# The first quarter's mixed rows are loaded and halved inside the attention, into the memory of q; the last samples' transpose moves behind the third unit of the output projection

## The chip, the core and the metric

The kernel runs on one core of one Trainium2 chip. The metric is the device time of one execution in microseconds (us). PE is the matrix engine, ACT, DVE and POOL are the scalar, vector and GpSimd engines, SP is the engine that issues most of the transfers (DMAs); ACT issues some of them too. Each engine works through its own instructions in order, and waits on semaphores for the others.

## The reference, cut

One decoder layer for a prompt of 1024 tokens and for 8 samples of 8 new tokens each, with a paged cache of 4096 tokens for every sample. The model width is 1024, the hidden width of the gated feed-forward part (FFN) 2816.

```
def trunk_layer(x, c, ...):
    mod = (jax.nn.silu(c) @ w_ada + b_ada)[:, None, :]
    shift1, scale1, gate1, shift2, scale2, gate2 = jnp.split(mod, 6, axis=-1)
    h = rms_norm(x, norm1) * (1 + scale1) + shift1
    z = h @ w_in                          # q, keys, values, gates, conv and pool inputs
    ...
    o_attn = (g[..., 0:1] * o_cmp + g[..., 1:2] * o_slc + g[..., 2:3] * o_win).reshape(B, T, ATTN_W)
    ...
    x = x + gate1 * (jnp.concatenate([o_attn, y_conv, y_pool], axis=-1) @ w_out)
    h = rms_norm(x, norm2) * (1 + scale2) + shift2
    x = x + gate2 * swiglu(h, w_up, w_down)
    return x, new_kv, win_state, u_ext[:, -CONV_BUF:], p_ext[:, -POOL_BUF:]
```

`o_cmp`, `o_slc` and `o_win` are three attentions (compressed, selected blocks, window). The change concerns the line with `w_out`, and what is ahead of it.

## The kernel before

Tokens lie along the free dimension: 1024 of the prompt and 64 of the samples, T = 1088, cut into four quarters of HALF = 272 (c = 0 to 3). Features lie on the 128 partitions, in KT = 8 blocks (k for inputs, m for outputs).

A product of full precision is made from three fast ones (`mm3`): each factor is halved into a rounded `hi` and the rest `lo`, and hi·hi, hi·lo and lo·hi are summed. `split` halves: a copy on ACT gives hi, a subtraction on DVE (or POOL) gives lo. So every weight and every activation costs work on ACT and on DVE before PE can use it. `w_raw` is a loaded weight, `w_hi` and `w_lo` its halves; `b_hi` and `b_lo` are those of an activation.

The stages, with their place in the profiled execution: the conditioning (adaLN) and the first norm (to 44 us); a part for tokens that gives values and gates (`token_part`, to 77); the input projection (86 to 385); the attention of the prompt, with that of the sample pairs beside it (387 to 819); the output projection (834 to 930); FFN up and down (to the end).

The attention writes its output, the "mixed rows", to `mix_d` in main memory: the prompt's from `mo`, the samples' from `smo`. A pair p of samples ends in `sample_combine`: DVE sums into `co`, PE transposes it, DVE copies it to `smo`, and SP stores it into the last columns of `mix_d`, which belong to the last quarter. The prompt's attention reads the queries `q` (a tile in pool `zq`), halved into `qh` and `ql` by `query_parts` for one of NB = 8 query blocks at a time.

`output_projection` has three groups of quarters: c = 0; c = 1; and c = 2 and 3 together. In each group it goes through the 8 blocks m of output rows; I call one m for one quarter a unit. A unit is 24 matmuls. For each group and m a weight `w_raw` is loaded on SP (`load`), and halved (`split`) into `w_hi` and `w_lo` in two halves of 512. The mixed rows come by `fetch` (`mixc`, 2 blocks k in each transfer; c = 0 on SP, the others on ACT's queue), and `mix` halves them into `mh` and `ml`. The table `MIX` says after which unit how many are halved. `x_load` issues the loads of the residual's x into `x1a` (quarters 0 and 1) or `x1b` (2 and 3) on ACT's queue. After a unit DVE adds the residual (`residual`, into x1a or x1b), SP stores the row (`x_d`), and ACT squares it (`n_ss` or `n_t`) for the second norm. When a quarter's 8 units are done, `late_norm` norms it: a matmul with `mean_d`, `n_rs` with its table load on ACT, a reciprocal on DVE, a multiplication on DVE and a scaling on ACT for each block.

The order of instructions is made when the program is built. Tasks are generators; `run` takes the one with the lowest priority number among those that are due by its own clocks (`use` adds a planned cost to an engine's clock, `yield` gives the time from which the task may go on); `spawn` adds a task, `hold` waits for a condition. A scheduler behind it may still move instructions within what depends on what, so the order of an engine isn't that of the code. Memory comes from pools on a left and a right stack; an instruction that gets memory which another tile held waits for that tile's last use.

## Time and profile before

| | us |
|---|---|
| median of 3 runs | 1679.19 (1678.71 to 1679.51) |
| profiled execution | 1670.79 |
| its span | 1669.2 |
| granted clock of PE, mean | 0.975 |

A row of a timeline has the start in us, the duration in us, the engine, the line of the kernel, the operation, output and inputs, the shape, and how many like it stand in a row; in brackets is how long the engine stood idle just before, and what ended that. The engines' names with q (ACTq, SPq) mean the issue of a transfer. A row of a group of waits has the total, the number and the longest, in us. A row of windows has the stretch, its length, then the busy time of PE, of PE's weight loads, DVE, ACT and POOL, each with its number of instructions, then the granted clock of PE (1.00 is full), the share of the 16 DMA engines that is busy, and GB/s. Durations of PE's matmuls overlap a little, so their starts show the rate.

### The profile page before, as it was taken

Reading aid. Unit: us, or ns where it says so; the run is one execution under the profiler, and the core shown is the slowest. Engines: PE = TensorE matmul, PEld = TensorE weight load, DVE = VectorE, ACT = ScalarE, POOL = GpSimd, SP = SyncE. Lnnn points to the kernel's source line nnn. Section 1 sums busy time; section 2 is a strip of 40 time slices with the busy share of each in tenths; the row PEclk is TensorE's granted clock in tenths of the full one; section 3 lists DMA queues with packets and bytes.
Section 4 is the critical chain, followed back from the end, with each engine's and each line's share of the span. In section 5 each row is a group of like instructions: output and inputs, shape, how many; then the busy total and the mean of one; then the engine's idle time right before and its main releaser. Section 6 shows DMA issues by size and latency. Waiting matters only on the chain. (4 is left out here: it accounts for less than half of the span.)

```text
span 1669.2 us, 35421 instructions
## 1 busy us (share of the span) xinstructions
PE 1565.7 (94%) x12569; PEld 1390.4 (83%) x12569; DVE 1092.0 (65%) x2633; ACT 777.8 (47%) x1829; POOL 660.9 (40%) x789
## 2 busy tenths in 40 slices
PE   6998999997999899899599989999999999899998
PEld 2898897896777666566399989999999999899988
DVE  4713233887555566766589878777777775577695
ACT  3522114335766667666467534433334433344463
POOL 3120110114333223223003366554555554778695
PEclk9999999998999899999899999999999999999999
DMA  9575765325457363344696564346443345966553
GB/s 342 196 261 160 204 174 167 126 101 156 127 178 214 110 193 97 91 127 139 197 323 194 197 215 175 141 145 231 146 143 141 137 145 198 397 232 241 187 168 122
DMA packets 195025, 302.10 MB, mean 181 GB/s; under 512 B 26353, under 2 KB 131378, under 8 KB 194530
## 3 DMA queue, kind: packets, MB, share of 16 engines
q1 hardware_dynamic: 174978, 272.20, 49.4%
q0 software_dynamic: 5856, 16.24, 3.2%
q10 hardware_dynamic: 14016, 11.41, 2.2%
q8 instruction: 100, 1.64, 0.4%
q14 instruction: 75, 0.61, 0.1%
HBM read 233.43 MB, written 70.53 MB: 182 GB/s over the span
## 5 line engine op out<-in xcount | busy, mean ns | idle before, releaser
L139 PE MATMUL bank<-b_hi,w_hi 128*128 128x272 f32 x1232 | 351.4, 290 | 6.0 <-DVE f_g L1677 2.9
L139 PE MATMUL bank<-b_lo,w_hi 128*128 128x272 f32 x1232 | 353.7, 289 | 2.5 <-DVE b_lo L171 2.5
L139 PE MATMUL bank<-b_hi,w_lo 128*128 128x272 f32 x1232 | 348.8, 288 | 0.9 <-DVE w_lo L171 0.9
L139 PEld LDWEIGHTS bank<-b_hi,w_hi 128*128 128x128 f32 x1232 | 230.6, 189 | 9.2 <-ACT b_hi L175 3.8
L139 PEld LDWEIGHTS bank<-b_lo,w_hi 128*128 128x128 f32 x1232 | 232.8, 189 | 3.4 <-DVE b_lo L171 3.3
L139 PEld LDWEIGHTS bank<-b_hi,w_lo 128*128 128x128 f32 x1232 | 230.8, 189 | 1.1 <-DVE w_lo L171 1.1
L1136 POOL TENSOR_SCALAR P<-P,st 128x128 f32<-128x128 f32 (+10 forms) x192 | 108.9, 581 | 229.6 <-DVE st L1132 130.9
L171 DVE TENSOR_TENSOR w_lo<-w_raw,w_hi 128x512 fp32r<-128x512 f32 (+2 forms) x121 | 117.0, 975 | 67.3 <-ACT w_hi L175 66.6
L139 PEld LDWEIGHTS bank<-stream 128*128 128x128 f32 x1056 | 131.1, 203 | 29.0 <-issue 14.6
L171 POOL TENSOR_TENSOR w_s<-w_raw 128x512 f32<-128x512 f32 (+1 forms) x88 | 125.8, 1429 | 67.8 <-DVE w_lo L171 55.2
L139 PE MATMUL bank<-stream 128*128 128x128 f32 x1056 | 138.4, 290 | 11.4 <-DMA wada<-in_wada 6.0
L171 POOL TENSOR_TENSOR x<-x,d_m 128x272 f32<-128x272 f32 x144 | 126.6, 901 | 34.4 <-DVE x L1879 19.6
L175 ACT ACTIVATE w_hi<-w_raw 128x512 fp32r<-128x512 f32 (+2 forms) x122 | 80.7, 677 | 125.9 <-PE bank L139 84.1
L1126 ACT ACTIVATE P<-P,st 128x128 f32<-128x128 f32 (+12 forms) x192 | 112.6, 588 | 44.5 <-DVE st L1120 28.5
L139 PE MATMUL bank<-h_hi,w_hi 128*128 128x384 f32 (+1 forms) x384 | 130.0, 338 | 0.5 <-DVE mod L1024 0.5
L139 PE MATMUL bank<-g,w_hi 128*128 128x272 f32 x616 | 121.6, 293 | 5.7 <-DVE x L1879 5.5
L139 PE MATMUL bank<-h_hi,w_lo 128*128 128x384 f32 (+1 forms) x384 | 126.4, 329 | 0.0
L171 DVE TENSOR_TENSOR w_lo<-w_s,w_hi 128x512 fp32r<-128x512 f32 (+1 forms) x124 | 116.3, 940 | 14.6 <-ACT w_hi L175 12.6
L139 PE MATMUL bank<-h_lo,w_hi 128*128 128x384 f32 (+1 forms) x384 | 125.7, 327 | 0.0
L139 PE MATMUL bank<-g,d_hi 128*128 128x272 f32 x616 | 120.3, 292 | 4.2 <-DVE x L1879 3.1
L1879 DVE SCALAR_TENSOR_TENSOR x<-bank,mod,x 128x272 f32<-128x272 f32 (+1 forms) x192 | 87.0, 476 | 38.3 <-PE bank L139 33.9
L139 PEld LDWEIGHTS bank<-g,w_hi 128*128 128x128 f32 x616 | 98.1, 191 | 7.3 <-DVE x L1879 6.1
(373 smaller groups left out, 3720.9 us busy)
## 6 DMA issues: line engine op xcount, KB each, us to landing
g_d<-f_s SPq DMA_DIRECT2D x57, 544.0 KB, 3.1
g<-g_d SPq DMA_DIRECT2D x56, 544.0 KB, 6.1
wada<-in_wada SPq DMA_DIRECT2D x96, 256.0 KB, 5.3
stream<-in_cacheA SPq DMA_DIRECT2D x192, 128.0 KB, 3.2
w_raw<-in_wup SPq DMA_DIRECT2D x40, 512.0 KB, 4.4
unit<-in_cacheB SPq DMA_DIRECT2D x152, 128.0 KB, 2.4
stream<-in_cacheB SPq DMA_DIRECT2D x104, 128.0 KB, 2.4
w_raw<-in_wout SPq DMA_DIRECT2D x24, 512.0 KB, 4.8
```

What stands on the lines that cost most here:

```text
L139: return self.nc.tensor.matmul(out, lhsT, rhs, start=start, stop=stop, skip_group_check=chain)
L171: (self.nc.vector if eng == "dve" else self.nc.gpsimd).tensor_tensor(out, a, b, op=op)
L175: self.nc.scalar.activation(hi, src, AF.Copy)
L1126: nc.scalar.activation(Ps, Ps, AF.Exp, scale=-1.0, bias=sy[:, g, 0:1], accum_out=sy[:, g, 1:2])
L1136: nc.gpsimd.tensor_scalar(Ps, Ps, sy[:, g, 3:4], 0.0, op0=OP.mult, op1=OP.add)
L1879: nc.vector.scalar_tensor_tensor(out[:, :n], acc[:, :n], self.mod[:, 5, m, 0:1], out[:, :n], op0=OP.mult, op1=OP.add)
```

## The change

One tile of 17,408 bytes on each partition, with the tag "q", now lies in a pool `base` that is open for the whole program, and serves in turn the first x (`x0`), the queries `q`, the mixed rows of the first quarter (`mix0`, both halves of 8 blocks), those of the third quarter (`mix2`), and from the third quarter's norm on the small tiles of the FFN (`hidden_space`: stores, sums and shares that had pools of their own).

A new task `first_mix` runs in the attention: when the last query block has been halved and the prompt's values have reached 14 units, it loads `mix0` in two transfers on SP and halves the 8 blocks. `output_projection` fetches quarters 1 to 3 only, the second on SP; it has 9 buffers of `mh` and `ml` where it had 17; the third quarter's rows go to `mix2`, in one go when the first quarter has been used. The transpose, copy and store of the last sample pair (`sample_store`, with `co` and `smo` in `base`) come after the third unit (m = 2) of the first quarter. The adaLN weights have 14 buffers, before 16. Pools in `tail` are opened in another order.

```diff
@@ -892,9 +892,8 @@
             yield from self.token_part(tp, h)
-        zq_ = self.pool("zq", "left")
-        self.q = zq_.__enter__().tile([P, 4, T], F32, name="q")
-        self.zout = (zq_, zp_)
+        self.q = self.big("q").rearrange("p (r t) -> p r t", r=4)
+        self.zout = (zp_,)
         order = ["kc", "vc", "cg0", "ch0", "bg0", "cg1", "ch1", "bg1", "p0", "ks", "p1", "kw", "q0", "q1", "q2", "q3"]
@@ -1057,6 +1056,7 @@
         self.split(*self.qs, self.q[:, :, j * P:(j + 1) * P], 512)
+        self.q_parts = j + 1
@@ -1422,23 +1422,29 @@
             nc.vector.tensor_scalar(w[:, a:b], w[:, a:b], ds_[:, 2 + x:3 + x], None, op0=OP.mult)
-        o = pool.tile([P, P], F32, name="co", bufs=2)
+        o = pool.tile([P, P], F32, name="co", bufs=2) if p < 3 else self.co
         nc.vector.tensor_scalar(o, part[:, 11], gr[:, 0:1], None, op0=OP.mult)
...
             nc.vector.scalar_tensor_tensor(o, part[:, c], w[:, c:c + 1], o, op0=OP.mult, op1=OP.add)
-        yield self.use("dve", 4.0, self.t["pe"]) + 0.5
-        tr = yield from self.bank_of("S")
+        r = self.use("dve", 4.0, self.t["pe"]) + 0.5
+        if p < 3:
+            yield r
+            tr = yield from self.bank_of("S")
+            self.sample_store(p, tr, o, pool.tile([P, 4, 2, NT], F32, name="smo", bufs=2))
+            self.give("S", self.t["dve"])
+        self.combined = p + 1
+
+    def sample_store(self, p, tr, o, mo):
+        nc = self.nc
         self.tr(tr[:, 0:P], o)
-        mo = pool.tile([P, 4, 2, NT], F32, name="smo", bufs=2)
         for g in range(2):
...
                 tr[s, 0:P].rearrange("p (b g r t) -> p g b r t", b=2, g=2, r=4)[:, g])
-        self.give("S", self.use("dve", 0.4, self.t["pe"]))
+        self.use("dve", 0.4, self.t["pe"])
         nc.sync.dma_start(self.mix_d[:, 0:4, SEQ + 16 * p:SEQ + 16 * p + 16],
                             mo.rearrange("p r b t -> p r (b t)"))
-        self.combined = p + 1
@@ -1459,6 +1465,23 @@
         self.spawn(lambda: 2 + 1.1 * self.u_done / 36, self.sample_attention(sp))
+        self.spawn(1.95, self.first_mix())
+
+    def first_mix(self):
+        nc = self.nc
+        yield from self.hold(lambda: self.q_parts == NB and self.v_done >= 14)
+        mix = self.big("mix0", F32R).rearrange("p (k x t) -> p k x t", k=KT, x=2)
+        for k in range(0, KT, 4):
+            nc.sync.dma_start(mix[:, k:k + 4, 1].bitcast(F32), self.mix_d[:, k:k + 4, 0:HALF])
+        at = self.use("dma", 3.0, self.t["pe"]) + 2.5
+        yield at
+        for k in range(KT):
+            hi, lo = mix[:, k, 0], mix[:, k, 1]
+            src = lo.bitcast(F32)
+            nc.scalar.activation(hi, src, AF.Copy)
+            r = self.use("act", 0.09 + HALF * 0.00084, at)
+            self.mix0.append((hi, lo, self.combine(lo, src, hi.bitcast(F32), OP.subtract, HALF, r, "dve")))
+            yield self.mix0[-1][2]
@@ -1473,6 +1496,9 @@
+    def big(self, name, dt=F32):
+        return self.base.tile([P, 4 * T], dt, name=name, tag="q", bufs=1)
+
     def halves(self, a):
@@ -1494,7 +1520,8 @@
         todo = [m for _ in groups for m in range(KT)]
-        raw, ws, mx, parts = [], [], [], {}
+        raw, ws, mx, mix2 = [], [], [], []
+        parts = {(0, k): a for k, a in enumerate(self.mix0)}
@@ -1505,33 +1532,36 @@
-        order = [(c, k) for c in range(4) for k in range(0, KT, 2)]
+        order = [(c, k) for c in range(1, 4) for k in range(0, KT, 2)]
...
                 t = pool.tile([P, 2, HALF], F32, name="mixc", bufs=4)
-                (nc.sync if c == 0 else nc.scalar).dma_start(t, self.mix_d[:, k:k + 2, c * HALF:c * HALF + HALF])
+                (nc.sync if c == 1 else nc.scalar).dma_start(t, self.mix_d[:, k:k + 2, c * HALF:c * HALF + HALF])
                 mx.append((c, k, t, self.use("dma", 0.8, self.t["pe"]) + 2.2))
...
                 c, k0, t, at = mx.pop(0)
+                if (c, k0) == (2, 0):
+                    mix2.append(self.big("mix2", F32R).rearrange("p (k x t) -> p k x t", k=KT, x=2))
                 for k in range(2):
-                    hi = pool.tile([P, HALF], F32R, name="mh", bufs=17)
-                    lo = pool.tile([P, HALF], F32R, name="ml", bufs=17)
+                    if c == 2:
+                        hi, lo = mix2[0][:, k0 + k, 0], mix2[0][:, k0 + k, 1]
+                    else:
+                        hi = pool.tile([P, HALF], F32R, name="mh", bufs=9)
+                        lo = pool.tile([P, HALF], F32R, name="ml", bufs=9)
                     r = self.split(hi, lo, t[:, k], HALF, at)
...
-        fetch()
         load()
-        for _ in range(3):
-            fetch()
         load()
         split()
-        mix(4)
         load()
+        for _ in range(4):
+            fetch()
         xq = [(c, k) for c in range(4) for k in range(4)]
@@ -1551,7 +1581,10 @@
                         wk = [self.halves(a)[:, k % 4] for a in w[k // 4][:2]]
-                        self.mm3(acc[:, :HALF], wk, parts[c, k][:2], k == 0, k == KT - 1)
+                        last = self.mm3(acc[:, :HALF], wk, parts[c, k][:2], k == 0, k == KT - 1)
+                    if c == 0 and m == 2:
+                        with self.tc.issue_after(last.ins):
+                            self.sample_store(3, self.bank(), self.co, self.smo)
                     if c == cs[-1]:
@@ -1565,9 +1598,22 @@
+    def hidden_space(self):
+
+        big = self.big("f_sT", F32R)
+        v = [big[:, 4 * HALF * x:4 * HALF * (x + 1)] for x in range(4)]
+        self.f_s = [a.rearrange("p (a b c) -> p a b c", a=2, b=2) for a in v[:3]]
+        self.f_T = [a.rearrange("p (a b) -> p a b", a=2).bitcast(F32) for a in (v[3][:, 0:2 * HALF], v[3][:, 2 * HALF:])]
+        self.f_U = [a.rearrange("p (a b) -> p a b", a=2).bitcast(F32) for a in (v[2][:, 0:2 * HALF], v[2][:, 2 * HALF:])]
+        self.x13 = {(c, h): v[2].bitcast(F32)[:, HALF * (2 * c + h):HALF * (2 * c + h + 1)] for c in range(2) for h in range(2)}
+        self.d_m = [big[:, HALF * n:HALF * (n + 1)].bitcast(F32) for n in range(6)]
+        self.b_t = [v[1].bitcast(F32)[:, HALF * n:HALF * (n + 1)] for n in range(3)]
+
     def late_norm(self, nt, ch, x1, ss, ready):
         nc = self.nc
+        if ch == 2:
+            self.hidden_space()
         c0, n = QUARTERS[ch]
@@ -2108,8 +2163,8 @@
                 self.ada_setup(ap)
-                begin(np_, 0, lambda: np_.tile([P, KT, CHUNKS[0][1]], F32, name="x0"))
-                ada = self.ada_rounds(ap, (1, 0), 16, nc.sync, "b")
+                begin(np_, 0, lambda: self.big("x0")[:, 0:KT * CHUNKS[0][1]].rearrange("p (k t) -> p k t", k=KT))
+                ada = self.ada_rounds(ap, (1, 0), 14, nc.sync, "b")
                 t = next(ada)
...
```

The rest of the diff gives other tiles their places in the shared memory (`hidden_space`: the FFN's stores, sums and shares, and x of the third quarter as the norm writes it) and opens pools in another order.

Three places show how the instructions move. The first is the start of the output projection, on PE from the attention's last matmuls on (`unit` is gathered keys or values of a sample, `spt` transposed weights of its softmax). Before:

```order
L143 MATMUL bank<-ident,e 128x128 x8
L139 MATMUL bank<-unit,spt 64x128 x16
L143 MATMUL bank<-ident,co 128x128
L139 MATMUL bank<-mh,w_hi 128x272 x5
L139 MATMUL bank<-ml,w_hi 128x272
L139 MATMUL bank<-mh,w_lo 128x272
L139 MATMUL bank<-mh,w_hi 128x272
```

and now (`mix_9074` is the tile mix0; the transpose of `co` stands 45 rows on, behind the third unit):

```order
L143 MATMUL bank<-ident,e 128x128 x8
L139 MATMUL bank<-unit,spt 64x128 x16
L139 MATMUL bank<-mix_9074,w_hi 128x272 x2
L139 MATMUL bank<-mix_9074,w_lo 128x272
L139 MATMUL bank<-mix_9074,w_hi 128x272 x2
L139 MATMUL bank<-mix_9074,w_lo 128x272
L139 MATMUL bank<-mix_9074,w_hi 128x272 x2
```

The output projection's matmuls follow the attention's, with mix0 in the place of mh and ml, and the transpose has gone from between them.

At the same place ACT, from the first weights of the output projection on. Before:

```order
L175 ACTIVATE w_hi<-w_raw 128x512 x2
L161 ACTIVATE part<-bank 128x128
L175 ACTIVATE w_hi<-w_raw 128x512 x7
L1540 DMA x1a_10498<-in_xT 128x2x272 x3
L175 ACTIVATE mh<-mixc 128x272 x2
L1540 DMA x1a_10498<-in_xT 128x2x272
L175 ACTIVATE mh<-mixc 128x272 x2
L1540 DMA x1a_10499<-in_xT 128x2x272
L1514 DMA mixc<-mix_d 128x2x272
L1540 DMA x1a_10499<-in_xT 128x2x272
```

and now:

```order
L175 ACTIVATE w_hi<-w_raw 128x512 x2
L161 ACTIVATE part<-bank 128x128
L175 ACTIVATE w_hi<-w_raw 128x512 x6
L1570 DMA x1a_10517<-in_xT 128x2x272 x4
L410 ACTIVATE n_ss<-x1a_10517 128x272
L175 ACTIVATE mh<-mixc 128x272 x4
L1570 DMA x1a_10518<-in_xT 128x2x272
L410 ACTIVATE n_t<-x1a_10517 128x272
L1570 DMA x1a_10518<-in_xT 128x2x272
L410 ACTIVATE n_t<-x1a_10517 128x272
L175 ACTIVATE mh<-mixc 128x272 x2
L175 ACTIVATE w_hi<-w_raw 128x512 x2
```

ACT's copy of the fifth unit's weights, the last row now, stands behind six issues of x1a, three squares (`n_ss`, `n_t`) of finished rows and six copies to mh. Before, nine weight halves stood together ahead of the issues and the copies to mh.

The second place is ACT where the second quarter begins. Before:

```order
L175 ACTIVATE mh<-mixc 128x272 x3
L1514 DMA mixc<-mix_d 128x2x272
L175 ACTIVATE mh<-mixc 128x272
L410 ACTIVATE n_t<-x1a_10498 128x272
L175 ACTIVATE w_hi<-w_raw 128x512 x2
L1514 DMA mixc<-mix_d 128x2x272 x2
L175 ACTIVATE w_hi<-w_raw 128x512 x2
L410 ACTIVATE n_ss<-x1a_10499 128x272
L175 ACTIVATE mh<-mixc 128x272
L1578 ACT_TABLE_LOAD
L1578 ACTIVATE n_rs<-bank,eps 128x272
```

and now (`mix_10959` is the tile mix2; the first row has the weights of the first quarter's last unit and of the second's first):

```order
L175 ACTIVATE w_hi<-w_raw 128x512 x4
L175 ACTIVATE mix_10959<-mixc 128x272 x8
L410 ACTIVATE n_t<-x1a_10517 128x272
L1541 DMA mixc<-mix_d 128x2x272
L175 ACTIVATE w_hi<-w_raw 128x512 x2
L1541 DMA mixc<-mix_d 128x2x272 x3
L410 ACTIVATE n_ss<-x1a_10518 128x272
L1624 ACT_TABLE_LOAD
L1624 ACTIVATE n_rs<-bank,eps 128x272
L1641 ACTIVATE x1a_10517<-x1a_10517,mod,s_129 128x272
L175 ACTIVATE w_hi<-w_raw 128x512 x2
```

Eight copies to mix2 stand in a row between the weights, and the norm's table load and n_rs come ahead of the weights in the last row. Before, the copies to mh were spread over the units.

The third is ACT in the attention (`P` and `e` are softmax weights of the prompt and of a sample, `cw` factors of a sample's parts, `pt` transposed P), as one piece of the difference:

```order
 L1378 ACTIVATE e,den<-e,nm 128x512
 L1417 ACTIVATE cw<-nm,cs 128x2
-L1126 ACTIVATE P,st<-P,st 128x55 x3
+L1481 ACTIVATE mix_9074<-mix_9074 128x272 x4
+L1126 ACTIVATE P,st<-P,st 128x55 x2
+L1481 ACTIVATE mix_9074<-mix_9074 128x272 x4
+L161 ACTIVATE pt<-bank 128x8x64
+L1126 ACTIVATE P,st<-P,st 128x55 x2
 L1126 ACTIVATE P,st<-P,st 128x896 x2
```

Eight copies to mix0 stand among the softmax steps of one query block; on DVE eight subtractions follow them.

At the start of the input projection, which isn't shown, the first loads of its weights (`w_raw<-in_win`) move on SP behind two loads of FFN weights that are prepared ahead (`p_raw`) and one store of their halves (`w_d`).

More of the change, by code (lines that the diff above doesn't have):

```diff
@@ L1614, in operands @@
         yield max(at) - 1.0
-        B = {(h, c): x1["at"](2 * p + c, i + 4 * h) for h in range(2) for c in range(2)}
+        B = {(h, c): x1["out"](2 * p + c, i + 4 * h) for h in range(2) for c in range(2)}
         B11, B12, B21, B22 = B[0, 0], B[0, 1], B[1, 0], B[1, 1]
@@ L2017, in tail @@
         p0 = p0_.__enter__()
+        xb_ = [self.pool(f"x1b{i}") for i in range(4)]
+        xb = {}
+        for i in (2, 1, 0, 3):
+            pool = xb_[i].__enter__()
+            xb[i] = pool.tile([P, 2, 2, HALF], F32, name="x1b")
         nt_ = self.pool("nt")
         nt = nt_.__enter__()
-        xb_ = [self.pool(f"x1b{i}") for i in range(4)]
-        xb = {}
-        for i in reversed(range(4)):
-            pool = xb_[i].__enter__()
-            xb[i] = pool.tile([P, 2, 2, HALF], F32, name="x1b")
+        bt_ = self.pool("bt")
+        bt = bt_.__enter__()
+        bt = [bt.tile([P, HALF], F32, name=f"b_t{n}") for n in range(3)]
         xa_ = self.pool("x1a")
@@ L2033, in x_load @@
             return xb[i][:, c - 2], xT[:, :, i, c * HALF:c * HALF + HALF]
-        x1 = {"load": x_load, "at": lambda c, k: xa[c][:, k] if c < 2 else xb[k % 4][:, c - 2, k // 4]}
+        at = lambda c, k: xa[c][:, k] if c < 2 else xb[k % 4][:, c - 2, k // 4]
+        x1 = {"load": x_load, "at": at, "out": lambda c, k: self.x13[c - 2, k // 4] if c > 1 and k % 4 == 3 else at(c, k)}
         def first_pair():
@@ L2145, in build @@
         self.constants()
+        self.base = self.ctx.enter_context(self.pool("base", "left"))
+        self.co = self.base.tile([P, P], F32, name="co3")
+        self.smo = self.base.tile([P, 4, 2, NT], F32, name="smo3")
         st_ = self.pool("stream", "left")
```

35 lines of the change are left out of this document (20 added, 15 removed).

## The prediction

> **What bounds the kernel.** The page comes first: which engine is full.
>
> ```profile
> span 1669.2 us, 35421 instructions
> PE 1565.7 (94%) x12569; PEld 1390.4 (83%) x12569; DVE 1092.0 (65%) x2633; ACT 777.8 (47%) x1829; POOL 660.9 (40%) x789
> ```
>
> PE bounds it with 94%, so a change that leaves its matmuls as they are can win only from the 103.5 us in which it stands, or from a slow clock. The profiled execution took 1670.79 us, 1.6 more than its span and 8.4 (0.5%) less than the median of 1679.19; my sum is a difference against the profiled execution, and I add it to the median. A change under 0.2% (3.4 us) can hardly be told from none here.
>
> Second, the waits of PE from 816 to 1000 us (total, times, longest):
>
> ```profile
> PE bank L139 <- ACT mh L175: 8.4, 1, 8.4
> PE bank L143 <- DVE co L1428: 6.9, 1, 6.9
> ```
>
> Two waits lead the list. PE's timeline shows that they stand side by side, where the attention ends and the output projection begins:
>
> ```profile
> 816.70 1.97 PE L139 MATMUL bank<-unit,spt 128*64 128x128 f32 x32 [0.65 <-DVE cs L1422]
> 825.54 0.47 PE L143 MATMUL bank<-ident,co 128*128 128x128 f32 x1 [6.87 <-DVE co L1428]
> 834.46 1.50 PE L139 MATMUL bank<-mh,w_hi 128*128 128x272 f32 x5 [8.45 <-ACT mh L175]
> 837.55 0.29 PE L139 MATMUL bank<-mh,w_hi 128*128 128x272 f32 x1
> ```
>
> From 818.67 to 834.46 PE does one transpose of 0.47: 15.3 us idle. What mh waits for is in ACT's timeline, with DVE's half of the first weights below, and the columns of the windows (PE, PEld, DVE, ACT, POOL, clock, DMA share, GB/s) show the price in clock:
>
> ```profile
> 818.07 1.15 ACT L175 ACTIVATE w_hi<-w_raw 128x512 fp32r<-128x512 f32 x2
> ...
> 823.87 1.15 ACT L175 ACTIVATE w_hi<-w_raw 128x512 fp32r<-128x512 f32 x2 [2.40 <-DMA w_raw<-in_wout]
> 833.97 0.43 ACT L175 ACTIVATE mh<-mixc 128x272 fp32r<-128x272 f32 x1 [6.79 <-DMA mixc<-mix_d]
> ```
> ```profile
> 818.74 0.68 DVE L171 TENSOR_TENSOR w_lo<-w_raw,w_hi 128x512 fp32r<-128x512 f32 x1
> ```
> ```profile
> 830.00:835.00 5.00, 0.54 (x2) 0.55 (x3) 0.56 (x2) 1.02 (x3) 0.00 (x0) 0.50 1.06 342
> 835.00:840.00 5.00, 5.00 (x33) 5.00 (x32) 2.57 (x7) 1.98 (x6) 0.00 (x0) 0.75 0.97 294
> 845.00:850.00 5.00, 5.00 (x42) 5.00 (x41) 3.98 (x9) 2.75 (x7) 0.00 (x0) 1.00 1.10 372
> 860.00:865.00 5.00, 5.00 (x42) 5.00 (x41) 4.99 (x13) 4.58 (x12) 0.00 (x0) 1.00 0.98 304
> 875.00:880.00 5.00, 4.66 (x37) 4.42 (x36) 5.00 (x12) 5.00 (x12) 0.00 (x0) 1.00 0.61 196
> 890.00:895.00 5.00, 3.94 (x29) 3.63 (x29) 4.86 (x11) 2.74 (x6) 0.00 (x0) 1.00 0.74 231
> ```
>
> The mixed rows come last, behind weights. After the gap the clock is 0.50, then 0.75. A warm window holds 42 matmuls in 5 us, 0.12 each, so a unit (one block of 128 output rows for one quarter: 24 of them) takes 3.0 us; the window at 0.75 has 9 fewer, and with the ten slow ones up to 837.55 I put the slow clock at 1.9. Before, the first quarter's eight units end at 834.46 + 1.9 + 24 = 860.4. Beyond that PE is full but for 0.34 and 1.06 (the windows at 875 and 890), DMA is full to 865, and DVE from 860: little there has slack.
>
> **The change, part by part.**
>
> *The gap goes.* Mixed rows of the first quarter are in memory, and the last samples' transpose stands behind the third unit. PE's first unit needs only w_hi (from 818.07) and w_lo (to 819.4; its first product is third in line): PE can start about 819.1, so 0.4 is left. Gain −15.3 −1.9 = −17.2; cost 0.4. The transpose's copy and store then have nobody on PE behind them until the third quarter.
>
> *The weights are next.* Weights for units 1 to 3 (counted from 0) come as before: the last at 823.87 + 1.15 = 825.0, while PE needs it at 819.1 + 9.0. Unit 3 ends, transpose included, at 831.5. In the new order ACT's half of unit 4's weights stands behind four issues of x1a, a square that needs unit 0's residual (so the first x1a must have landed), six copies to mh of the second quarter, and two more squares. Issue to landing of the transfers there (count, KB, median):
>
> ```profile
> w_raw<-in_wout SPq DMA_DIRECT2D x9, 512.0 KB, 4.6
> x1a<-in_xT ACTq DMA_DIRECT2D x8, 272.0 KB, 5.2
> x1b<-in_xT ACTq DMA_DIRECT2D x7, 272.0 KB, 7.0
> mixc<-mix_d ACTq DMA_DIRECT2D x6, 272.0 KB, 6.3
> ...
> mixc<-mix_d SPq DMA_DIRECT2D x4, 272.0 KB, 5.2
> ```
>
> 825.1 + 5.2 for x1a, 0.5 residual, 0.4 square, six copies and two squares at 0.35 to 0.43: 834.3 at the earliest, 836.2 if x1a lands in 7.0 as x1b does; with the half of 0.6, PE stands 3.4 to 5.4. I take 4.4. Unit 7 has the same trouble: on SP its w_raw stands behind four mixc, the finished rows of units 0 to 3 and the transposed output, and on ACT its w_hi stands behind eight x1b issues and a mixc, each of which waits for an earlier landing (5.2 to 7.0 apiece, overlapping). From 834.5 two rounds of these end at 847 to 848.5; units 4 to 6 end about 845: 3.8 (2 to 5). DMA's share above (1.06 to 1.10) says why I don't take the low end: the first quarter's 1.1 MB of mixc no longer loads here, which at 342 GB/s relieves 3.3 us, but x1a, x1b and weights want the same 16 engines 15 us sooner. So the first quarter ends 17.2 − 8.6 = 8.6 earlier, at T = 851.8.
>
> *The second quarter starts with a pile.* The third quarter's rows go into the shared memory, which the first quarter's occupy until T: sixteen halvings in one go, ahead of unit 1's weights on both ACT and DVE; and the first quarter's norm follows. Their rows today:
>
> ```profile
> 861.32 1.38 ACT L175 ACTIVATE mh<-mixc 128x272 fp32r<-128x272 f32 x4
> ...
> 866.29 1.28 ACT L1578 ACT_TABLE_LOAD   x1
> 867.58 0.49 ACT L1578 ACTIVATE n_rs<-bank,eps 128x272 f32<-128x272 f32 x1
> ```
> ```profile
> 861.53 0.49 DVE L1468 SCALAR_TENSOR_TENSOR x1a<-bank,mod,x1a 128x272 f32<-128x272 f32 x1
> ...
> 862.54 1.49 DVE L171 TENSOR_TENSOR ml<-mixc,mh 128x272 fp32r<-128x272 f32 x4
> ...
> 868.31 1.84 DVE L1581 RECIPROCAL n_rs<-n_rs 128x272 f32<-128x272 f32 x1
> ...
> 870.96 0.78 DVE L1587 TENSOR_TENSOR x1a<-x1a,n_rs 128x272 f32<-128x272 f32 x2
> ```
>
> Eight copies are 2 × 1.38 = 2.8 on ACT, eight differences 3.0 on DVE; then a square, w_hi, w_lo: unit 1 resumes at T + 4.7, where PE was ready at T + 3.0: 1.7. After its own w_hi (T + 4.2) ACT does a square, the table load and n_rs, to T + 6.4; DVE follows with the reciprocal to T + 8.2, seven multiplications (2.7) and a residual to T + 11.3, and only then with unit 2's w_lo: T + 11.7, where unit 1 ended at T + 7.5: 4.2. Unit 4 waits another 1.4 behind copies to b_hi. Sum 7.3 (bounds 1.4, if the norm's steps find room while PE works, and 9). Unit 4 then ends at T + 15 + 7.3 = 874.1 and before at 860.4 + 15 = 875.4: 1.3 of the 8.6 are left.
>
> *Clock.* Each new wait can slow what follows. The trace has two near rows, with the windows behind them:
>
> ```profile
> 692.48 1.21 PE L143 MATMUL bank<-ident,P 64*128 64x64 f32 x32 [2.60 <-POOL P L1136]
> 968.95 0.56 PE L139 MATMUL bank<-b_hi,w_hi 128*128 128x272 f32 x1 [2.95 <-DVE f_g L1677]
> ```
> ```profile
> 692.00:696.00 4.00, 3.48 (x52) 2.52 (x52) 2.58 (x10) 2.07 (x4) 0.43 (x1) 1.00 0.50 153
> 970.00:975.00 5.00, 5.00 (x27) 5.00 (x27) 4.69 (x8) 1.29 (x3) 4.62 (x7) 0.60 0.17 60
> ```
>
> After 2.60 the clock stays at 1.00; after 2.95 the window has 27 matmuls and not 42: 15 × 0.12 = 1.9 lost. Three of the new waits (4.4, 3.8, 4.2) are longer. Unit 4's loss is hidden, since unit 7 waits for a transfer anyway; unit 7's counts, 1.9; the second quarter's is hidden but for 0.5 by unit 4's wait of 1.4. I take +2.4, bounds 0 and 5.7 (all three). [...]
>
> *Later waits.* Of 0.34 + 1.06, which come of DVE and ACT being late, I count 1.0 as gone, since eight differences (3.0) have left DVE: −1.0, bounds −1.4 and 0.
>
> *Attention pays for the halving.* The two loads overwrite q, so they follow its last read:
>
> ```profile
> 675.94 0.69 DVE L171 TENSOR_TENSOR ql<-q,qh 128x512 fp32r<-128x512 f32 x1
> ```
> ```profile
> 679.08 0.28 ACT L1417 ACTIVATE cw<-nm,cs 128x2 f32<-128x2 f32 x1
> ```
>
> Issued at 676.6 and landed in about 4 (under w_raw's 4.6, as DMA is nearly idle here), they hold ACT from 679.4 to 680.6: 1.2. Then come eight copies (2.8) between softmax steps, and eight differences among DVE's steps that end in the wait of 2.60 above. DVE is full there, and DMA at 0.03:
>
> ```profile
> 684.00:688.00 4.00, 4.00 (x36) 2.73 (x34) 3.96 (x17) 4.00 (x11) 1.50 (x3) 0.59 0.03 6
> ```
>
> DVE comes some 3.4 late (3.0 and a little waiting). PE's wait for POOL grows by 0.5, if this work fills waits of ACT and DVE, to 4.0, if all of it and part of the load's landing reach PE; I take 2.1, near the middle. Nothing gives it back, as PE goes on in order.
>
> *Input projection.* Its first weight loads lie in other memory now, wait for the token part's last matmuls, and stand behind two p_raw and one w_d on SP. PE has other work meanwhile:
>
> ```profile
> 77.35 4.63 PE L139 MATMUL bank<-c_peT,stream 128*128 128x2 f32 x32
> 81.84 4.95 PE L139 MATMUL bank<-stream 128*128 128x128 f32 x22
> 86.53 0.43 PE L139 MATMUL bank<-h_hi,w_hi 128*128 128x384 f32 x1
> ```
>
> Issued at 77.4, landed in 4.6 as w_raw's row above, halved in about 2.3 (ACT's two halves take 1.15, and DVE as long): 84.3. PE needs them at 86.53, and 1.6 later still, since seven more of the 22 transposes of 4.95 now stand ahead. Cost 0; bounds 0 and +4, if a w_d ahead lands late.
>
> The adaLN weights' 14 buffers instead of 16, hidden_space's fixed places for tiles that had pools, and the removal of pool zq leave PE's work; I take 0 ± 1.
>
> Sum: −17.2 + (0.4 + 4.4 + 3.8) + 7.3 + 2.4 − 1.0 + 2.1 + 0 = +2.2, so 1673.0 for the profiled execution and 1681.4 for the median.
>
> **The rivals.**
>
> *Half of the new waits only.* If x1a lands in 4.6 or less, unit 4 waits 2 and unit 7 1, and clock costs 0.5, attention its low end 0.5, the second quarter still 7.3: −17.2 + 3.4 + 7.3 + 0.5 − 1.0 + 0.5 = −6.5, 1673. For it: 1.1 MB less to move. Against: DMA at 1.06.
>
> *The whole gain stays.* The planner's order is harmless since DVE and ACT start their piles while PE is busy; second quarter 1.4: −17.2 + 0.4 + 1.4 + 2.1 − 1.0 = −14.3, 1665. For it: ACT is busy only 2.75 of 5 us at 845. Against: the transfers' landing times.
>
> *Slower: the clock falls after every new wait.* The place is units 4 and 7, unit 2 of the second quarter, and the attention's POOL wait grown from 2.60 to 4.7. Price: 5.7 + 1.9 instead of 2.4, so +7.4: 1686.6. It decides when these waits pass 2.95 with nothing behind that waits anyway. For it: the row at 968.95; against: later transfers hide part. [...]
>
> *Slower: the input projection waits.* Decided when the halves are later than 88.1, that is, with a landing of over 8 us: +2.2 + 4, 1685.4. Against: 4.6 above.
>
> *The gap stays,* because the early rows or the first weights come late after all: no gain and no waits in the first quarter, 7.3 − 1.0 + 2.1 = +8.4, 1688. Weights ready at 819.1 speak against it.
>
> **How the numbers follow.** Base case 0.42, 1681.4, rounded to 1681 (own range 1677 to 1685); half of the waits 0.22; whole gain 0.15; clock 0.11; input projection 0.07; gap stays 0.03. Faster by over 0.2% (under 1675.8): 0.20 of the second case and the 0.15: 0.35. Slower (over 1682.6): 0.10 of the base, 0.11, 0.07, 0.03: 0.31. The rest 0.34. The range leaves out the whole gain and the gap that stays, and takes the other ends: 1669 to 1687.
>
> **What would show it.** Right: no wait of over 1 us before the first matmul with mix; waits for w_hi or w_lo of 3 to 5 us some 12 us and 25 us later, and of 4 us in the second quarter; clock under 0.8 after them; a wait for POOL of 4 to 5 near 692. Wrong: PE full from 819 to 860, which would make it much faster; or a wait for the first input projection's weights near 86.

## The result, and the profile after

The changed kernel takes 1690.27 us (median of 7 runs, 1685.69 to 1694.20) beside 1678.71 for the kernel before (7 runs, 1671.17 to 1680.22): a ratio of 1.0074, 95% interval [1.0051, 1.0097]. Run again, beside 27 runs of the kernel before on the chip of the last experiments, it took 1687.96 beside 1675.08, 1.0079 [1.0056, 1.0102]. It is 12 to 13 us slower, where I had said +2.2.

The profiled execution took 1693.83 us, 3.6 above its median, and that of before 1670.79 lay 4.3 under the median of 27 later runs (1675.08; lowest 1669.33, highest 1684.40). So these two traces lie 23.0 us apart, some 10 us more than the kernels do, and I read every place in a second profile of the changed kernel (1687.42 us) too. The page, first and second profile:

```profile
span 1692.2 us, 35415 instructions
...
PE 1585.9 (94%) x12569; PEld 1401.9 (83%) x12569; DVE 1082.3 (64%) x2631; ACT 779.0 (46%) x1830; POOL 662.6 (39%) x790
```
```profile
span 1685.8 us, 35415 instructions
...
PE 1578.4 (94%) x12569; PEld 1395.8 (83%) x12569; DVE 1084.3 (64%) x2631; ACT 779.9 (46%) x1830; POOL 663.3 (39%) x790
```

PE's matmuls are as many as before. It stands idle for 106.3 and 107.4 us, before 103.5: taking the gap of 15.3 us away left PE as idle as it was. The rest of the time lies in PE's busy time, in part because its mean clock is lower (0.968 and 0.972, before 0.975). By the starts of landmarks in PE's timelines (us):

| stretch | before | changed, 1st | changed, 2nd |
|---|---|---|---|
| to the token part's first matmul | 44.65 | 49.28 | 48.50 |
| to the input projection | 41.9 | 43.5 | 42.0 |
| input projection and attention | 732.1 | 741.1 | 737.1 |
| output projection | 116.4 | 121.3 | 121.7 |
| FFN | 734.2 | 737.1 | 736.5 |

The place of the change, PE's timeline, in the first profile and then in the second:

```profile
831.89 1.97 PE L139 MATMUL bank<-unit,spt 128*64 128x128 f32 x32 [0.65 <-DVE cs L1422]
...
834.68 0.39 PE L139 MATMUL bank<-mix,w_lo 128*128 128x272 f32 x1 [0.21 <-DVE w_lo L171]
...
850.50 0.82 PE L139 MATMUL bank<-mix,w_hi 128*128 128x272 f32 x2 [3.68 <-ACT w_hi L175]
868.61 0.82 PE L139 MATMUL bank<-mix,w_hi 128*128 128x272 f32 x2 [5.79 <-ACT w_hi L175]
877.75 0.39 PE L139 MATMUL bank<-mh,w_hi 128*128 128x272 f32 x1 [0.61 <-ACT w_hi L175]
...
883.92 0.39 PE L139 MATMUL bank<-mh,w_hi 128*128 128x272 f32 x1 [1.94 <-ACT w_hi L175]
885.87 0.39 PE L139 MATMUL bank<-mh,w_lo 128*128 128x272 f32 x1 [1.44 <-DVE w_lo L171]
```
```profile
825.62 1.97 PE L139 MATMUL bank<-unit,spt 128*64 128x128 f32 x32 [0.65 <-DVE cs L1422]
...
844.15 0.82 PE L139 MATMUL bank<-mix,w_hi 128*128 128x272 f32 x2 [3.60 <-ACT w_hi L175]
862.41 0.82 PE L139 MATMUL bank<-mix,w_hi 128*128 128x272 f32 x2 [6.22 <-ACT w_hi L175]
```

The gap is gone: 0.21 us are left of it. Unit 4 waits 3.68 and 3.60, unit 7 waits 5.79 and 6.22, both for ACT's half of the weights. What the waits cost in clock (the columns as in the prediction):

```profile
849.00:854.00 5.00, 3.28 (x12) 2.79 (x13) 5.00 (x13) 3.97 (x10) 0.00 (x0) 0.54 1.09 374
854.00:859.00 5.00, 5.00 (x33) 5.00 (x33) 2.82 (x6) 1.33 (x3) 0.00 (x0) 0.77 1.01 330
...
869.00:874.00 5.00, 5.00 (x25) 4.77 (x25) 2.09 (x4) 1.12 (x3) 0.00 (x0) 0.57 0.78 242
```

At 0.12 us apiece, 15, 9 and 17 matmuls are missing beyond the idle time. ACT ahead of unit 7's weights, and the transfers there with count, KB and median us to landing:

```profile
858.82 0.43 ACT L410 ACTIVATE n_t<-x1a 128x272 f32<-128x272 f32 x1 [2.99 <-issue]
...
862.87 0.43 ACT L410 ACTIVATE n_t<-x1a 128x272 f32<-128x272 f32 x1 [3.62 <-DMA x1b<-in_xT]
862.90 4.67 ACTq L1570 DMA_DIRECT2D x1b<-in_xT  x3
867.61 0.43 ACT L410 ACTIVATE n_t<-x1a 128x272 f32<-128x272 f32 x1 [4.31 <-DMA x1b<-in_xT]
867.95 2.17 ACT L175 ACTIVATE w_hi<-w_raw 128x512 fp32r<-128x512 f32 x4
```
```profile
x1a<-in_xT ACTq DMA_DIRECT2D x8, 272.0 KB, 6.1
x1b<-in_xT ACTq DMA_DIRECT2D x8, 272.0 KB, 6.8
mixc<-mix_d SPq DMA_DIRECT2D x4, 272.0 KB, 7.5
```

From 859.25 to 867.95 ACT computes two squares of 0.43 and no more. Three issues of x1b hold its queue for 4.67 us until earlier x1b have landed, and the halving behind them comes the moment they let go. DMA is full meanwhile (a share of 1.06). Landing takes 6.1 us for x1a (5.2 before), 6.8 for x1b (7.0 before) and 7.5 for mixc on SP (5.2 before).

### The profile page after: what moved, and what is told of

Same layout as the page of the kernel before. It is cut to its first block, busy times and chain, and to the rows that moved or that the text cites. A ratio compares the mean times of both kernels' runs of the same rounds, so it can differ in the third digit from the quotient of the medians.

```text
span 1692.2 us, 35415 instructions
## 1 busy us (share of the span) xinstructions
PE 1585.9 (94%) x12569; PEld 1401.9 (83%) x12569; DVE 1082.3 (64%) x2631; ACT 779.0 (46%) x1830; POOL 662.6 (39%) x790
## 4 chain that ended last, share of the span: by engine, by line
PE 65%; DVE 12%; ACT 6%; DMA 6%; issue 5%; POOL 3%; SPq 1%; ACTq 0%; DVEq 0%; POOLq 0%
PE bank L139 62%; PE bank L143 3%; ACT P L1126 2%; DVE P L1114 2%; DVE w_lo L171 1%; DMA w_raw<-in_wup 1%; POOL w_s L171 1%; DMA w_raw<-in_wout 1%; POOL x L171 1%; DMA x1b<-in_xT 1%; DVE co L1428 1%; ACT w_hi L175 1%; POOL f_sT L171 1%; DMA stream<-in_wtok 1%; DMA wada<-in_wada 1%
## 5 line engine op out<-in xcount | busy, mean ns | idle before, releaser
L1136 POOL TENSOR_SCALAR P<-P,st 128x128 f32<-128x128 f32 (+11 forms) x192 | 109.4, 584 | 229.1 <-DVE st L1132 107.7
L139 PEld LDWEIGHTS bank<-stream 128*128 128x128 f32 x1056 | 135.9, 209 | 30.1 <-issue 17.0
L139 PE MATMUL bank<-stream 128*128 128x128 f32 x1056 | 143.3, 296 | 12.2 <-DVE pre L551 5.5
L171 POOL TENSOR_TENSOR x<-x,f_sT 128x272 f32<-128x272 f32 x144 | 127.3, 906 | 38.3 <-DVE x L1928 27.6
L1126 ACT ACTIVATE P<-P,st 128x640 f32<-128x640 f32 (+12 forms) x192 | 112.7, 588 | 44.1 <-DVE st L1120 28.3
```

The lines of the kernel that those rows point to most:

```text
L139: return self.nc.tensor.matmul(out, lhsT, rhs, start=start, stop=stop, skip_group_check=chain)
L171: (self.nc.vector if eng == "dve" else self.nc.gpsimd).tensor_tensor(out, a, b, op=op)
L1126: nc.scalar.activation(Ps, Ps, AF.Exp, scale=-1.0, bias=sy[:, g, 0:1], accum_out=sy[:, g, 1:2])
L1136: nc.gpsimd.tensor_scalar(Ps, Ps, sy[:, g, 3:4], 0.0, op0=OP.mult, op1=OP.add)
```

## The experiments

All ratios are against runs of the kernel before on the same chip (its medians there 1675.1 to 1675.2). A stretch's time is that of one profile; only ratios have intervals.

**Changed kernel, the residual's loads of the last two quarters later.** `x_load` issues x1b only in the second quarter, behind ACT's last halving copy.

```
-                    x_load()
+                    if cs[0] == 0:
+                        x_load(2 if xq and xq[0][0] < 2 else 0)
+                    else:
+                        with self.tc.issue_after(self.last_act.ins):
+                            x_load()
```

> The changed kernel, with the loads of x1b (third and fourth quarter) issued on ACT in the second quarter, behind its weight halves, and not in the first. Theory B2 (the first quarter's second wait, 5.8 us, is made by x1b: its issues hold ACT, and its 2.2 MB hold the DMA engines, while the last units' weights are needed): that wait falls under 1.5, no long wait comes in its place, and the time falls by 4 to 6 from the changed kernel, ratio to before 1.004. Rival C (what is won there is given back in the second quarter, as with x on POOL's queue, where a wait of 9.5 came up): a wait of 5 or more in the second quarter, and at most 1 us less, ratio 1.007.

1678.42, ratio 1.0016 [1.0002, 1.0031]: some 10 us of the 12 to 13 are gone, more than the 4 to 6 expected. PE's timeline, and the windows of both waits:

```profile
846.85 0.82 PE L139 MATMUL bank<-mix,w_hi 128*128 128x272 f32 x2 [3.15 <-ACT w_hi L175]
861.03 0.52 PE L139 MATMUL bank<-mix,w_hi 128*128 128x272 f32 x2 [1.57 <-ACT w_hi L175]
```
```profile
845.00:850.00 5.00, 2.93 (x10) 2.44 (x11) 5.00 (x13) 4.31 (x11) 0.00 (x0) 0.65 1.08 379
...
860.00:865.00 5.00, 3.76 (x28) 3.54 (x29) 3.54 (x6) 3.56 (x7) 0.00 (x0) 1.00 0.71 210
```

Unit 4's wait stays, since x1a and mixc are still ahead of it; unit 7's falls from 5.79 to 1.57. The output projection takes 110.8 us, not 121.3: 10.5, of which 4.4 to unit 7 (30.3 us behind the attention's end, before the edit 34.8) and the rest later; the FFN gives 2.7 to 3.3 of it back (739.8 us). Single waits differ between executions, so all profiles count here. With x1b early (the two above, and the run by tiles below, whose output projection is the same) the first quarter takes 40.1, 40.0 and 36.7 us and the rest of the output projection 81.1 to 81.7; with x1b late (this run and two below that have it) they take 33.9 to 34.8 and 76.9 to 77.2. That the early x1b makes most of the loss is shown, in the first quarter and behind it.

**Changed kernel, x1a and x1b issued on POOL's queue.** The rival was that ACT's queue alone is to blame, and not what the 16 DMA engines have to carry.

```
-                nc.scalar.dma_start(dst, src)
+                nc.gpsimd.dma_start(dst, src)
```

> The changed kernel, with the loads of x1a and x1b issued on POOL's queue and not on ACT's; ACT's order then has ten weight halves in a row where six stood ahead of the loads. Theory B (the first quarter's two waits of 3.7 and 5.8 us, and the slow clock behind them, come from weight halves that stand on ACT behind the issues of x and the squares): both waits shrink under 1.5, the first quarter takes some 28 us and not 39.5, and the time falls by 8 to 12, to 1679 to 1682. Rival C (the transfers themselves are the limit there, and the waits turn into waits for landed weights): at most 3 less, 1687 or more.

1687.18, 1.0070 [1.0052, 1.0089]: nothing gained that this can tell. The waits of the first quarter fell to 0.66 and 0.49, and it took 27.5 us, as theory B had it; but a larger wait came in the second quarter, and the time is rival C's. PE, then ACT and SP there:

```profile
866.79 0.59 PE L139 MATMUL bank<-mh,w_hi 128*128 128x272 f32 x1 [9.53 <-ACT w_hi L175]
```
```profile
860.74 4.95 ACTq L1541 DMA_DIRECT2D mixc<-mix_d  x4
865.79 0.43 ACT L410 ACTIVATE n_ss<-x1a 128x272 f32<-128x272 f32 x1 [4.66 <-DMA w_raw<-in_wout]
866.12 1.13 ACT L175 ACTIVATE w_hi<-w_raw 128x512 fp32r<-128x512 f32 x2
```
```profile
858.23 0.33 SPq L1515 DMA_DIRECT2D w_raw<-in_wout  x1
```

Now four mixc hold ACT for 4.95 us, and the unit's weights were issued only at 858.23. The wait has moved, the bytes to load are the same, and the DMA engines' share is 0.98 to 1.07 in the windows from 845 to 860, where it was 0.98 to 1.09 in the changed kernel.

**Changed kernel, the last transpose at its old place.** The sample pair's transpose and store again follow its sums.

```
-                    if c == 0 and m == 2:
-                        with self.tc.issue_after(last.ins):
-                            self.sample_store(3, self.bank(), self.co, self.smo)
...
```

> The changed kernel, with the last samples' transpose at its old place, ahead of the first unit. Theory D (weights and x set the pace of the first quarter, so PE's start matters little): PE stands some 7 us before the first unit again, the first quarter's two waits shrink by about as much, and the time rises by 0 to 3 from the changed kernel. Rival (the wait adds to the others): 6 to 8 more.

1685.12, 1.0065 [1.0049, 1.0080], not to be told from the changed kernel. PE waits ahead of the output projection instead:

```profile
831.79 0.48 PE L143 MATMUL bank<-ident,co 128*128 128x128 f32 x1 [6.83 <-DVE co L1428]
```

Behind it no wait over 0.21 is left in the first quarter: in that time, by my reading, the loads land and ACT gets ahead. So the wait for the sums and the waits for weights stand for each other. In its profile the output projection takes 114.3 us, 7 less than in the changed kernel, and the FFN 742.5, 5 to 6 more; of the 7 nothing sure is left in the time.

**Kernel before, the transpose behind the third unit.** This part of the change alone.

> The kernel before, with only the transpose, copy and store of the last samples moved behind the third unit of the first quarter (their two tiles, 768 bytes, in the pool of constants). Theory D: the first quarter's rows are issued on SP some 2 us earlier, as they no longer stand behind the samples' store, the gap before the first unit is 12 to 13 us instead of 15, and the time falls by 1 to 2. Rival (the rows come late because DMA is full, not because of the queue): no change.

1677.27, 1.0012 [0.9995, 1.0029]. The gap shrinks to 12.57, as expected, but the time doesn't fall: what the gap saves is lost in the second quarter (30.6 us, before 25.1). PE, DVE's run of multiplications of the norm, and a window there:

```profile
830.32 1.05 PE L139 MATMUL bank<-mh,w_hi 128*128 128x272 f32 x3 [12.57 <-ACT mh L175]
```
```profile
867.82 4.23 DVE L1596 TENSOR_TENSOR x1a<-x1a,n_rs 128x272 f32<-128x272 f32 x7
```
```profile
870.00:875.00 5.00, 2.96 (x20) 2.74 (x20) 5.00 (x13) 4.58 (x10) 0.69 (x1) 0.90 0.22 68
```

The seven multiplications stand ahead of weights that PE needs: 20 matmuls in a window for 42. This is one part of the pile that the prediction saw in the changed kernel; the other, the copies to mix2, doesn't exist here.

**Kernel before, only the late loads of x1b.** The same edit as in the first experiment, made to the kernel before.

> The kernel before with the residual's loads of the third and fourth output block held back into the second quarter; nothing else. Theory (they only hurt where the first quarter has other loads to land): before has its gap of 15.3 us for the mixing tiles, which are loaded in it, and with less beside them they land 1 to 2 us sooner: ratio 0.9988 to 1.0000. Rival (the gap is set by the place of the mixed rows' load in the program alone): 0.9995 to 1.0005.

1679.08, 1.0023 [1.0007, 1.0040]: a loss, if a small one. The output projection is as before (116.1, before 116.4; gap 6.77 and 8.16). So x1b's early loads cost nothing in the kernel before; their price comes with an earlier start of the first quarter, as the next run shows too. The whole is 1.2 to 6.7 us slower, where 0 to 2 us faster was expected. In this profile the FFN takes 739.7 us (734.2 to 737.0 in the other five of the kernel before and its variants), and why isn't shown: the next run has the late loads too, and 734.5.

**Kernel before, both of these.**

> The kernel before with the last samples' transpose and store behind the third unit, and the residual's loads of the third and fourth output block held back. Theory (with the transpose alone the mixing tiles took 7 to 9 us to land beside the residual's rows): the gap of 12.57 us falls to 7 to 9 us, ratio 0.9970 to 0.9990. Rival (the rest of the FFN gives it back as in the run with the transpose alone): 1.0000 to 1.0015.

1670.03, 0.9957 [0.9936, 0.9977]: faster than both kernels, though each edit by itself gained nothing. PE at the gap, and the window nearest to the place of the one above (this attention ended 7.5 us later):

```profile
837.48 1.05 PE L139 MATMUL bank<-mh,w_hi 128*128 128x272 f32 x3 [12.28 <-ACT mh L175]
```
```profile
875.00:880.00 5.00, 5.00 (x42) 5.00 (x41) 5.00 (x13) 5.00 (x12) 0.80 (x1) 1.00 0.71 231
```

The gap is 12.28, so the 7 to 9 us that I had expected is wrong: the mixed rows come no sooner. What changed is the second quarter (24.5 us), with 42 matmuls where 20 stood: the output projection takes 112.1 us, with the transpose alone 121.2. When the norm's first multiplication starts, 26 weight halves (`w_lo`, two for each unit's weights) of the output projection are done on DVE and POOL; with the transpose alone 22, in the kernel before 25. So with the early x1b the norm's pile finds fewer weights in hand, and PE waits for the next ones.

**Kernel before, 14 adaLN buffers.** Loads go ahead in rounds of four tiles (`bufs // 4`), so 14 buffers give three rounds where 16 gave four.

```
-                ada = self.ada_rounds(ap, (1, 0), 16, nc.sync, "b")
+                ada = self.ada_rounds(ap, (1, 0), 14, nc.sync, "b")
```

> The kernel before, with one number changed: 14 buffers for the adaLN weights, not 16, so that three rounds of four loads run ahead and not four. Theory A (the shorter lookahead is what delays the front by the 4.6 us that the two profiles show at the first token matmul, 44.65 and 49.28): about +4.6, 1683; the first token matmul near 49. Rival (the front is late because the new shared tile and its waits lie there): no change, 1679, first token matmul at 44 to 45.

1677.72, 1.0012 [0.9998, 1.0026], that is +2.0 us, −0.3 to +4.4. PE's first matmul of the token part, before and with 14 buffers, and the window from 25 to 50 us of each:

```profile
44.65 0.39 PE L139 MATMUL bank<-wt_hi,h_hi 128*128 128x280 f32 x1 [1.79 <-ACT h_hi L472]
```
```profile
48.89 0.39 PE L139 MATMUL bank<-wt_hi,h_hi 128*128 128x280 f32 x1 [2.83 <-ACT h_hi L472]
```
```profile
25.00:50.00 25.00, 20.45 (x119) 11.11 (x114) 24.18 (x34) 13.17 (x26) 7.18 (x6) 0.93 1.01 364
```
```profile
25.00:50.00 25.00, 18.37 (x110) 7.31 (x109) 15.26 (x26) 9.38 (x18) 7.16 (x6) 1.00 0.75 255
```

DMA, which is full in that window before, falls from 364 to 255 GB/s. In all profiles with 16 buffers this matmul starts at 44.65 to 46.54 (five), in all with 14 at 47.16 to 49.71 (nine); the means differ by 2.6. By the start of the input projection the two sets are 85.94 to 86.53 and 87.37 to 93.18, and the means differ by 4.1.

**Changed kernel, the adaLN's loads ahead by tiles.** If three rounds in place of four are the cause, going ahead by single tiles (14 tiles, not 12) gives some of it back; `tiles(n)` issues the next n.

```
-            for i in range(ahead):
-                load(i)
+            tiles(bufs)
...
-            load(i + ahead)
+            tiles(4)
```

> The changed kernel, with the adaLN weights loaded ahead tile by tile, so that all 14 buffers are used and not 12. Theory A (lookahead): 2 to 4.6 us less than the changed kernel, 1686 to 1688, first token matmul at 45 to 47. Rival (shared tile): as the changed kernel, 1690.

1684.32, 1.0059 [1.0044, 1.0074], with an interval that overlaps the changed kernel's. The matmul starts at 48.53, as late as without. The edit neither shows nor excludes that the rounds matter; what is seen is the effect of the two buffers.

Behind the front this is the changed kernel, so its profile is a third execution of the output projection. Unit 4 waits 3.29 there, but unit 7 only 3.09, and the output projection takes 118.4 us:

```profile
858.98 0.52 PE L139 MATMUL bank<-mix,w_hi 128*128 128x272 f32 x2 [3.09 <-ACT w_hi L175]
```

**Kernel before, the early load and halving of the first mixed rows, unused.** `first_mix` in the attention, in q's memory; the output projection as before.

> The kernel before, with the new task in the attention added: two loads of the first quarter's mixed rows and sixteen halvings in the memory of q, whose results nobody uses (the output projection still loads and halves the first quarter itself). It prices the attention's part alone. Theory A: PE's end of the attention moves by 1.9 to 3.4 us, and so does the time: 1681 to 1682. Rival (the halving hides in the waits of ACT and DVE, and what the two profiles show there is chance): under 0.5.

1677.85, 1.0021 [1.0006, 1.0035]: 3.5 us, 1.0 to 5.9, where 1.9 to 3.4 was expected. Input projection and attention take 736.4 us in its profile (from 86.36 to 822.71); the five without the halving average 735.1, from 731.5 to 739.3, so that one profile can't show the difference.

**Changed kernel, late x1b, adaLN by tiles, and mix2's copies in pairs.** The copies to mix2 are each held behind a halving copy of ACT, so that they don't stand eight in a row.

```
+                    if cs[0] == 1 and m < 7:
+                        with self.tc.issue_after(self.last_act.ins):
+                            mix(MIX[cs[0], m])
```

> The changed kernel with three repairs: adaLN weights ahead by 14 tiles, x1b in the second quarter, and the third quarter's halvings pinned in pairs behind the weight halves of the second quarter's units. Theories A and B2 with the pile of halvings priced at 2: 2.5 + 5 + 2 less than the changed kernel, ratio to before 1.001 to 1.002. Rival C: 2.5 less, ratio 1.005 to 1.006.

1678.52, 1.0020 [1.0010, 1.0031], the same as with late x1b alone, and in the range that was expected of all three repairs together. The output projection took 111.6 (110.8 there). The pile of copies isn't worth anything that shows once x1b is out of the way.

**Changed kernel, late x1b, adaLN by tiles, and the first rows' copies spread.** Each of the eight copies in the attention is held behind a later exponential, and the planner sets them 9 us apart.

```
-            nc.scalar.activation(hi, src, AF.Copy)
+            with self.tc.issue_after(self.att_ins.ins):
+                nc.scalar.activation(hi, src, AF.Copy)
...
-            yield self.mix0[-1][2]
+            yield max(self.mix0[-1][2], self.t["pe"] + 9.0) if k < KT - 1 else self.mix0[-1][2]
```

> The changed kernel with the residual's loads of the third and fourth output block held back into the second quarter, the modulation's loads ahead counted by tile (14 buffers used, not 12), and the eight halvings of the first mixing tile each pinned behind a later exponential of the attention, so that no two follow one another. Theory (the halvings stand in front of the exponentials that the P tiles wait for): the attention gets back 2 to 3.5 us, POOL's P waits in the attention fall under 1.2 us mean, ratio 0.9995 to 1.0005. Rival (the halvings cost their ACT time wherever they stand, since ACT has no slack there): ratio 1.0015 to 1.0025, as with the two other edits alone.

1677.46, 1.0017 [1.0002, 1.0031]: the rival's number. The profile does show shorter waits for P from 490 to 830 us, first the changed kernel (second profile), then this one:

```profile
PE bank L143 <- POOL P L1136: 9.0, 5, 2.6
```
```profile
PE bank L143 <- POOL P L1148: 7.1, 4, 2.6
```

PE's waits for `st` (the minima and sums of the softmax's rows, on DVE) fall from 9.3 to 5.1 there as well, and input projection and attention take 735.0 us, where the other seven profiles of the changed kernel and its variants have 736.9 to 741.1. So the attention gets back some 2 us in this profile, as the theory had it; the time doesn't show it, since that is less than the interval (±2.5 us) can tell, and this stays open.

**The changed kernel once more.**

> The changed kernel once more, on the chip of these runs: ratio 1.006 to 1.009, and with the second profile the same waits in the first quarter (3 to 4 us and 5 to 6 us on halved weights) if they belong to the kernel and not to one execution. If they were of one execution only, they differ by over 2 us each and the ratio falls under 1.005.

1.0079 [1.0056, 1.0102]. Its rows stand with the result above. The places of the waits belong to the kernel; the size of unit 7's wait doesn't (6.22 here, 5.79 and 3.09 in two other executions).

## Why the prediction was wrong, by its steps

*The gap goes:* right. 0.21 us are left, where 0.4 was forecast.

*The weights are next:* right in place and releaser, wrong in size for unit 7. Unit 4 waits 3.68 and 3.60 (forecast 4.4). Unit 7 goes on 34.8 us after the attention's end in both profiles (868.61 − 833.86, 862.41 − 827.59); by the prediction it goes on at 848.8, one unit ahead of T, which is 30.1 after the attention's end of before (818.67). The term "3.8 (2 to 5)" failed by 4.7 us. Its working took two rounds of landings on ACT's queue. The x1b went out in three groups, at 855 to 859, at 862 and up to 867.6, the later ones held until earlier ones had landed, at nearly 7 us a landing. In the third execution the last three issues held ACT for 2.34 us, not 4.67, and unit 7 went on at 31.7: the miss is 1.6 to 4.7 us. By the starts of the second quarter's first matmuls, the first quarter ends 40.1 and 40.0 us after the attention (36.7 in the third execution), with 33.1 forecast and 41.3 before: of the 17.2 us of the gap with its clock, 1.2 are left in the two profiles (4.6 in the third), and not 8.6.

*The second quarter starts with a pile,* and *later waits:* the sum came out right, the cause was another, and that is luck. From the first quarter's end to the FFN it takes 81.1 and 81.7 us, before 75.1: +6.0 and +6.6, forecast 7.3 + 0.5 − 1.0 = 6.8. But PE's waits at the start of the quarter are 0.61, 1.94 and 1.44, not 1.7, 4.2 and 1.4, with a lower clock behind them (0.80 and 0.86 in the windows from 884 to 894); with x1b late the stretch takes 76.9 us, so that some 4.5 of the 6 come with x1b's early loads, which this step's forecast left out: when the norm's first multiplication starts, 20 weight halves are done in the first profile and 26 with x1b late. The copies to mix2, spread, gave nothing that shows (77.0).

*Clock:* the drop after the waits came as said (0.54 and 0.57). That unit 4's loss is hidden, because unit 7's weights would have come no sooner, is argued and not tried. The reading that a wait of 2.60 leaves the clock full holds for that row alone: the profile of before has a wait of 2.63 with a clock of 0.63 behind it (in the last section).

*Attention pays for the halving:* 2.1 forecast. Input projection and attention take 2.3 us more in the mean of the nine profiles with the halving than in that of the five without, but each set spreads by 6 to 8 us; the run of that part alone is 3.5 us slower [1.0, 5.9]. The size is one that these runs allow, the row is wrong, so the mechanism isn't confirmed. The wait for P that was to grow from 2.60 to 4 or 5 stands at 1.74 in the changed kernel, and its row moved by 16.8, of which 8.8 lie ahead of the attention (387.4 to 396.2):

```profile
709.25 1.22 PE L143 MATMUL bank<-ident,P 64*128 64x64 f32 x32 [1.74 <-POOL P L1136]
```

PE waits for DVE's `st` instead. From 490 to 830 us these waits sum to 4.3 to 6.3 us in the five profiles without the halving and to 7.0 to 9.8 in eight with it (all but the one with spread copies), while those for P fall from 11.3 to 11.9 down to 7.7 to 9.9.

*adaLN's buffers, hidden_space: 0 ± 1:* failed on both. The token part starts 4.6 and 3.9 us later in the two profiles (2.6 by the means of all), the input projection 6.2 and 4.0 (4.1 by the means). I hadn't looked at what limits the first 50 us: DMA's share there is 1.01 (from 25 to 50). The two missing buffers take load from it, as the run with 14 buffers shows in its window, and +2.0 us in time, short of certain. In the FFN, the up part takes from its first to its 1500th matmul 200.9 to 202.8 us in the six profiles of before and its variants, 203.6 to 207.2 in the eight with the shared memory. PE's waits there, before and then in the second profile of the changed kernel:

```profile
PE bank L139 <- DVE f_g L1677: 2.9, 1, 2.9
PE bank L139 <- DVE b_lo L171: 2.5, 3, 0.8
PE bank L139 <- DVE w_lo L171: 0.9, 1, 0.9
```
```profile
PE bank L139 <- DVE b_lo L171: 4.8, 5, 1.6
PE bank L139 <- ACT f_m L1728: 1.2, 1, 1.2
PE bank L139 <- DVE w_lo L171: 1.2, 1, 1.2
```

All waits together are 6.7 before and 8.5 now: +1.8 us, and the stretch is 2.7 longer. Halves of the second pair (`b_lo`) come later. Whether the shared memory does that, or the order of the work, wasn't tried.

*Input projection:* its weights didn't make PE wait. It starts 1.6 and 0.1 us further behind the token part.

In sum for the second profile: start +4.0, input projection and attention +5.0 (against an attention of before that was 3.0 under the mean of its kind), output projection +5.3 (+2.0 in the third execution), FFN +2.3, so 16.6; less those 3.0, 13.6, where the runs have 13.2 (9.4 to 17.1). The prediction had 0, +2.1, +0.1 and 0. Of the rivals none was it; "the gap stays" came nearest, at 1688 by the price of its other terms, for another reason: the gap was taken away and came back as waits. The range ended too low because I never let two slow ends come together.

What stays open: the FFN's cause, the share of the adaLN's loads by rounds, and the late loads' loss in the kernel before. Open too is why unit 7's wait differs by 3 us between executions of the same output projection. The parts don't simply add up: late x1b takes 10 us from the changed kernel, and nothing else that was tried takes anything sure from the 2.7 that are left. In the profiles of the changed kernel's variants the FFN takes 738.7 to 742.5 us, in its own 736.5 and 737.1, so that part of what a variant wins ahead of the FFN is lost in it, and why isn't shown.

## What to carry to other kernels

Before a gap on the full engine is closed, add up what has to land in the time that the gap gave: here 15.3 us of standing were also 15.3 us in which weights, mixed rows and residual rows landed (the DMA engines' share was 0.80 in the gap and 1.04 in its last 5.7 us), and without the gap the work behind waited for halved weights instead (3.68 and 5.79 us), until the loads that nobody needed yet (x1b) were moved out. The transpose behind the third unit and the late x1b gained nothing singly and 0.43% together: an edit that takes a wait away may need the next one's cure before it pays. ACT, which both computes and issues transfers here, had its computing held behind issues that waited (4.67 us by three of x1b, 4.95 by four of mixc); look in such a queue for who stands behind whom. Cost the harmless-looking parts of a change too (two buffers fewer, a shared tile) by what limits the stage in which they lie.
